# Moving an output projection's operand onto the finished scan's memory in a one-layer encoder trunk

## The chip, the cores and the metric

The kernel runs on one core of one Trainium2 chip. The metric is the device time of one execution in microseconds (us). The kernel before was timed three times: 1633.44, 1635.32 and 1642.16 us, a median of 1635.32 us. On this core TensorE (PE in the profile, with its weight loads as PEld) does the matrix products, VectorE (DVE), ScalarE (ACT) and GpSimd (POOL) do the elementwise work, and SyncE (SP) issues every DMA of this kernel from one queue. Each engine takes its instructions strictly in the order in which they were written into its stream, and waits at the first one whose inputs are not there.

## What is computed

One layer of a bidirectional encoder trunk on 1024 tokens of 1024 numbers, all in float32. Cut to what matters here:

```
h    = rms_norm(x) ; proj = h @ w_in
attn = window_attention(rope(q), rope(k), v)          # 512 of the mixer's 1024 columns
dn   = gated_deltanet(q, k, v, gate, decay, beta)     # the other 512, forward + backward scan
x    = x + rms_norm(concat(attn, dn) @ w_out)         # the output projection of the mixer
x    = x + rms_norm(cross_attention(rms_norm(x), mem) @ w_co)
gu   = rms_norm(x) @ w_gate_up
x    = x + rms_norm((silu(gate) * up) @ w_down)
```

Products are made to nearly float32 accuracy out of a fast matrix format: an operand is split into a rounded part `hi` and a remainder `lo`, and three products (hi·hi, hi·lo, lo·hi) are summed. The split is two instructions: a cast on ACT (`whi`, `b`, `s` ... at L102) and a subtraction on DVE or POOL (L103).

## The kernel before, in words

The program has three parts. The first makes all projections of the mixer and prepares the scans. The second (up to L934) runs the two delta-rule scans of 8 steps each, and around them, in an order written out by hand (`ORDER_3`), 16 windows of attention (8 blocks of 128 tokens for each of two groups of heads) and the keys and values of the memory tokens. Its last entries are windows and values: a window's scores (`psw`, L633) go through DVE (L635, maximum), ACT (L642, exponential; L650, scaling), a transposition on PE (`ptw`, L656), a split (`ph`, `pl`) and the product with the values (`pow`, L661), and its result `ao` is stored to the DRAM array `d_mix` (L666). The scans store their half of `d_mix` at L848. The values are products `pcv` (L907), copied out by ACT as `vv` (L911; that tile has one buffer) and stored to `d_mv` (L912).

The third part starts with the output projection of the mixer (`mid_gemm`, L994). It is done in two halves of 512 tokens (`hf` 0 and 1). Each half is 192 products of 512 columns in two chunks of columns; a chunk uses four blocks of `w_out`, 24 products each, and a block is loaded (`wraw`), cast (`whi`) and subtracted (`wlo`) in tiles that have two buffers each. The left operand of a half is `d_mix`, loaded in four blocks of 256 rows (`mraw`, L1033; block 0 and 1 are the two groups of the window attention, 2 and 3 the scans) and split into `b` tiles. Half 0 needs windows 0 to 3 of both groups, half 1 windows 4 to 7.

Where a tile lies decides when it can be written: a tile that is laid over another waits for the other's readers. The big operand tiles of part three (16 KB a partition each) lie in a pool `opB` (`b0`, `b1`, `b2`), in `opB3` (`b3`) on the left side of the memory, and in `opA` (`s00`, `s01`) on the right side, where the scans' tiles (pool `t3`) lay. In the kernel before, half 0 of the mixer's operand is `b1`, `b2`; its raw blocks 2 and 3 lie in `opA`, but raw blocks 0 and 1 lie in a separate pool `raw01` (L947) on the left, over memory that the windows use. Half 1 is `b0`, `b3`, its raw blocks in `opA`. The accumulators of the projection (`pg3`, four banks of PSUM) lie on the right side, where the windows' banks were, and two pools of two banks (`pn3`, `px3`) on the left, where the scans' and values' banks were.

A scheduler orders the instructions of each engine: it places them by its own estimate of when each could run, and weight loads are put ahead by `high_priority`. So moving a tile changes not only waits but the order in all five streams.

Behind the projection come the cross attention (`pcq`, `pcs`, `pco`), its output projection (the same `mid_gemm`), then the feed-forward part: 11 steps, each for two blocks of 128 gate columns and the same of up columns (index `i` 0 and 1), where products A, B, D, E of 12 matmuls each (L1165) are combined so that fewer products are needed. The last products of a step are the late ones, one each of A, D and E for both `i`; behind each of them `quarter` (L1235 to L1244) adds on DVE, takes the silu on ACT or multiplies by it on POOL. The down projection (`pd`) ends the kernel.

Of the kernel before, what the change touches and what calls it, by code (L numbers as in the profile page):

```python
# [10 lines left out]
F32 = mybir.dt.float32  # L11
F32R = mybir.dt.float32r
# [4 lines left out]
PSUM = bass.MemoryType.PSUM  # L17
DRAM = bass.MemoryType.DRAM

P = 128  # L20
S = 1024
D = 1024
KT = D // P
NT = S // P
HALF = 512
# [50 lines left out]
def tile_hybrid_block(  # L76
# [31 lines left out]
    def pool(name, bufs, **kw):  # L108
        return tc.tile_pool(name=name, bufs=bufs, reuse_waits="tile", **kw)
# [824 lines left out]


    p3 = ExitStack()
    pg = p3.enter_context(pool("pg3", 4, space=PSUM, side="right"))
    pn = p3.enter_context(pool("pn3", 2, space=PSUM))
    px = p3.enter_context(pool("px3", 2, space=PSUM))
    L0 = ExitStack()  # L940
    LX = ExitStack()
    opB = LX.enter_context(pool("opB", 1))
    b0, b1, b2 = (f"b{i}" for i in range(3))
    s2_first = [None] + [opB.tile([P, KT, HALF], F32R, tag=t, name=t) for t in (b0, b1, b2)]
    LR = ExitStack()
    raw01 = LR.enter_context(pool("raw01", 1)).tile([P, KT // 2, HALF], F32, name="mraw")
    LR.close()  # L947
    opB3 = LX.enter_context(pool("opB3", 1))
    opA = LX.enter_context(pool("opA", 1, side="right"))

# [72 lines left out]

    tz = L1.enter_context(pool("tz", 1))
    gp = gpost_tile(tz, g_mix_post)
    mxT = [s2_first[2:], [s2_first[1], opB3.tile([P, KT, HALF], F32R, tag="b3", name="b3")]]

    raws = [opA.tile([P, KT, HALF], F32, tag=f"s0{i}", name="mraw") for i in range(2)]
    for hf in range(2):
        for kp in range(4):  # L1030
            k2 = slice(2 * kp, 2 * kp + 2)
            raw = raw01 if hf == 0 and kp < 2 else raws[hf]
            nc.sync.dma_start(raw[:, k2, :], d_mix[kp * 256:(kp + 1) * 256, hf * HALF:(hf + 1) * HALF]  # L1033
                              .rearrange("(k p) t -> p k t", p=P))
            split(mxT[hf][0][:, k2, :], mxT[hf][1][:, k2, :], raw[:, k2, :])
    xn0 = mid_gemm(tz, mxT[0], w_out, gp, x, d_x1, 0)
    h2T = [operand(opA, "s0")]
    xn1 = mid_gemm(tz, mxT[1], w_out, gp, x, d_x1, 1, between=lambda: turn_norm(xn0, "cross", *h2T[0], pin=True))
    h2T.append(operand(opB, "s1"))
    turn_norm(xn1, "cross", *h2T[1])  # L1040

    mtp = L1.enter_context(pool("mtp", 1))
# [8 lines left out]
    tx = L2.enter_context(pool("tx", 2))  # L1051

    def cross_q(hf):
        q = operand(*((opB, "s2") if hf == 0 else (opA, "s0")))
        for ct in range(KT):
            whi, wlo = load_w(w_cq[:, ct * P:(ct + 1) * P], KT, P, nc.gpsimd)
            pp = [pg.tile([P, 512], F32, tag="pg", name="pcq")]
            gemm_b(whi, wlo, h2T[hf:hf + 1], pp)
            split(q[0][:, ct, :], q[1][:, ct, :], pp[0])
        return q  # L1060
# [60 lines left out]
    def blocks(t):  # L1121
        return t[:, 0:HK], t[:, HK:KT]

    xn = mid_gemm(tz, q0, w_co, gp, d_x1, d_x2, 0)
    x1h, x1l = operand(opB, "s1")
    X11, X21 = (x1h[:, 0:HK], x1l[:, 0:HK]), (x1h[:, HK:KT], x1l[:, HK:KT])

    def turned_k(xn, k):
# [7 lines left out]
        nc.scalar.activation(raw[:, k, :], pt, AF.Identity, scale=gain("ffn", k))  # L1136
        split(x1h[:, k, :], x1l[:, k, :], raw[:, k, :], eng=nc.gpsimd)
    xn = mid_gemm(tz, q1, w_co, gp, d_x1, d_x2, 1)
    T2, T4 = (blocks(t) for t in operand(opB, "s2"))
    T1, T3 = (blocks(t) for t in operand(opA, "s0"))  # L1140
    for k in range(HK):
        p0, p1 = turned_k(xn, k), turned_k(xn, k + HK)
        g0, g1 = gain("ffn", k), gain("ffn", k + HK)
# [28 lines left out]
    for e in range(EARLY):  # L1172
        f = 2 * e
# [74 lines left out]
    for f in range(0, NF, 2):  # L1248
        early = f // 2 < EARLY
        wts = [pair_weights(c0, early) for c0 in (f * P, FF + f * P)]  # L1250
        act = {(r, hf): tg.tile([P, HALF], F32, tag=f"act{r}{hf}", name=f"act{r}{hf}", bufs=1)
               for r in range(2) for hf in range(2) if not (early and r == hf == 0)}
        st = []
        for i, (W1, W22, (S1, S2, S3, S4)) in enumerate(wts):
            a1, v, u = (tg.tile([P, 512], F32, tag=n, name=n) for n in ("a1", "v", "u"))
            A = None
            if early:
                nc.sync.dma_start(a1, d_m1[f + i])
            else:
                A = bank("pA")  # L1260
                product(A, W1[0], X11)
                nc.scalar.copy(a1, A)
            B_, D_, E_ = (bank(n) for n in ("pB", "pD", "pE"))
            product(B_, S2, T2)
            nc.vector.tensor_tensor(v, a1, B_, ALU.add)
            product(D_, S1, T1)
            nc.vector.tensor_tensor(u, v, D_, ALU.add)
            product(E_, S3, T3)
            quarter(i, act, 1, 1, u, E_)
            st.append((A, D_, E_, v))  # L1270
        for i, (W1, W22, (S1, S2, S3, S4)) in enumerate(wts):
            A, D_, E_, v = st[i]
            if A is not None:
                product(A, W1[1], X21, start=False)
                quarter(i, act, 0, 0, None, A)
            product(D_, S4, X22, start=False)
            quarter(i, act, 0, 1, v, D_)
            product(E_, W22, T4, start=False)
            quarter(i, act, 1, 0, v, E_)
        for (r, hf), o_ in act.items():  # L1280
            nc.sync.dma_start(d_act[f + r][:, hf * HALF:(hf + 1) * HALF], o_)
# [99 lines left out]
```

## Time and profile before

The profiled execution took 1637.34 us on the device; its span, from the first instruction to the last, is 1635.6 us, so 1.7 us lie around it. It is 2.02 us above the median of the three timed runs.

| part of the span (us) | what runs | PE busy | granted clock |
|---|---|---|---|
| 400 to 560 | scans, windows, memory keys | 150.45 of 160.00 | 0.98 |
| 560 to 640 | last windows, memory values, start of the projection | 62.18 of 80.00 | 0.89 |
| 640 to 900 | projection, cross attention, second projection | nearly all | 0.94 to 1.00 |
| 1000 to 1100 | start of the feed-forward part | 97.42 of 100.00 | 1.00 |
| 1400 to 1636 | down projection | 227.40 of 236.00 | 0.99 |

In the lines of the profile each row of a timeline is a start, a duration, engine, line, operation, output and inputs, and in brackets the time for which the engine stood idle before it and what ended that. "Granted clock" is the share of full TensorE clock that the chip gave in a stretch; at 0.5 every product takes twice its time. The chain of waits is followed back from the last instruction, so whatever stands in it delayed the end.

### The profile page before, as it was taken

The numbers are of one execution on the slowest core, as the hardware profiler recorded it, in microseconds if no ns is written. First come the engines' busy times: TensorE is split into PE (matmuls) and PEld (weight loads), VectorE is DVE, ScalarE is ACT, GpSimd is POOL, SyncE is SP. The second block draws the span as 40 slices with busy tenths as digits, with TensorE's granted clock in tenths as the row PEclk, the third lists the DMA queues.
The fourth block names the chain that finished last, engine by engine and source line by source line (L and its number), as shares of the span: only waits on it lengthen the run. The fifth ranks groups of instructions, "written<-read, shape, count | busy, mean of one in ns | idle before, by whom it ended". The sixth has DMA issues, their size and how long they took to land.

```text
span 1635.6 us, 21442 instructions
## 1 busy us (share of the span) xinstructions
PE 1554.2 (95%) x7690; PEld 1301.3 (80%) x7690; DVE 942.7 (58%) x1431; ACT 750.8 (46%) x1518; POOL 548.9 (34%) x501
## 2 busy tenths in 40 slices
PE   6999889999899978999999999999999999999997
PEld 5878778777799857788888777888888888888886
DVE  6855986966668745443346458776555553334332
ACT  6556552237768764554336565233333232444211
POOL 2467553334337400253202221343333441321100
PEclk9999999898999998999999999999999999999999
DMA  6134257574999593454223164442223223565452
GB/s 201 41 116 130 64 166 208 140 181 133 320 320 289 149 293 112 151 184 146 74 65 116 52 213 151 126 135 77 78 90 96 79 84 114 202 214 183 140 175 73
DMA packets 267815, 240.47 MB, mean 147 GB/s; under 512 B 43176, under 2 KB 216637, under 8 KB 267709
## 3 DMA queue, kind: packets, MB, share of 16 engines
q1 hardware_dynamic: 267709, 239.11, 47.2%
q8 instruction: 60, 0.98, 0.3%
q14 instruction: 46, 0.38, 0.1%
HBM read 177.69 MB, written 58.75 MB: 145 GB/s over the span
## 4 chain that ended last, share of the span: by engine, by line
PE 67%; DVE 9%; DMA 6%; issue 3%; ACT 3%; POOL 2%; SPq 1%; POOLq 0%; ACTq 0%; DVEq 0%
PE pmg L994 10%; PE pd L1335 8%; PE pd L1311 7%; PE pE L1165 7%; PE pD L1165 7%; PE pA L1165 6%; PE pcq L260 5%; PE pB L1165 3%; PE psc L763 3%; PE pcs L1074 1%; PE pg L260 1%; DVE acc L285 1%; PE pco L1100 1%; PE pow L661 1%; DVE tmpb L510 1%
## 5 line engine op out<-in xcount | busy, mean ns | idle before, releaser
L102 ACT CAST whi<-wraw 128x1024 fp32r<-128x1024 f32 x108 | 113.4, 1050 | 167.3 <-issue 60.0
L103 POOL TENSOR_TENSOR wlo<-wraw,whi 128x1024 fp32r<-128x1024 f32 x48 | 118.3, 2464 | 174.4 <-ACT whi L102 156.1
L260 PE MATMUL pg<-hhi,whi 128*128 128x512 f32 x352 | 141.7, 404 | 0.2 <-ACT hhi L102 0.2
L260 PE MATMUL pg<-hlo,whi 128*128 128x512 f32 x352 | 141.5, 402 | 0.0
L260 PE MATMUL pg<-hhi,wlo 128*128 128x512 f32 x352 | 141.4, 402 | 0.0
L994 PE MATMUL pmg<-whi,b 128*128 128x512 f32 x384 | 119.8, 402 | 15.2 <-ACT b L102 12.6
L103 DVE TENSOR_TENSOR wlo<-wraw,whi 128x1024 fp32r<-128x1024 f32 x60 | 74.6, 1245 | 92.6 <-ACT whi L102 88.4
L1165 PE MATMUL pA<-b,whi 128*128 128x512 f32 x352 | 109.5, 392 | 1.4 <-ACT m L1182 1.4
L994 PEld LDWEIGHTS pmg<-whi,b 128*128 128x128 f32 x384 | 73.4, 193 | 32.1 <-ACT b L102 13.4
L285 DVE SCALAR_TENSOR_TENSOR acc<-cp,cols,acc 128x1024 f32<-128x1024 f32 x48 | 75.6, 1576 | 34.3 <-ACT acc L283 33.6
L1242 POOL TENSOR_TENSOR act<-act,up 128x512 f32<-128x512 f32 x33 | 48.4, 1468 | 106.6 <-issue 57.0
L260 PEld LDWEIGHTS pg<-hhi,wlo 128*128 128x128 f32 x352 | 68.0, 193 | 13.6
L260 PEld LDWEIGHTS pg<-hhi,whi 128*128 128x128 f32 x352 | 67.8, 193 | 13.5 <-ACT hhi L102 0.4
L260 PEld LDWEIGHTS pg<-hlo,whi 128*128 128x128 f32 x352 | 67.9, 193 | 13.3
L1165 PEld LDWEIGHTS pA<-b,whi 128*128 128x128 f32 x352 | 65.3, 188 | 15.1 <-ACT m L1182 2.0
L994 PE MATMUL pmg<-wlo,b 128*128 128x512 f32 x192 | 71.3, 392 | 0.0
L1165 PE MATMUL pA<-b,wlo 128*128 128x512 f32 x176 | 68.7, 391 | 1.1 <-DVE wlo L103 1.1
L1335 PE MATMUL pd<-wdh,ath 128*128 128x512 f32 x176 | 69.4, 395 | 0.0
L1335 PE MATMUL pd<-wdh,atl 128*128 128x512 f32 x176 | 69.4, 395 | 0.0
L1335 PE MATMUL pd<-wdl,ath 128*128 128x512 f32 x176 | 69.4, 395 | 0.0
L1311 PE MATMUL pd<-dl,whi 128*128 128x512 f32 x176 | 68.5, 389 | 0.0
L1311 PE MATMUL pd<-dh,wlo 128*128 128x512 f32 x176 | 68.3, 389 | 0.0
(392 smaller groups left out, 4145.0 us busy)
## 6 DMA issues: line engine op xcount, KB each, us to landing
wraw<-in_w_gate_up_dram SPq DMA_DIRECT2D x52, 512.0 KB, 3.9
kv<-d_kv SPq DMA_DIRECT2D x32, 512.0 KB, 7.1
wraw<-in_w_in_dram SPq DMA_DIRECT2D x22, 512.0 KB, 4.2
araw<-d_act SPq DMA_DIRECT2D x22, 512.0 KB, 3.4
draw<-in_w_down_dram SPq DMA_DIRECT2D x22, 512.0 KB, 4.3
atr<-d_act SPq DMA_DIRECT2D x16, 704.0 KB, 4.8
d_act<-act SPq DMA_DIRECT2D x40, 256.0 KB, 2.3
d_kv<-kv SPq DMA_DIRECT2D x8, 1024.0 KB, 6.4
```

The lines of the kernel that those rows point to most:

```text
L102: nc.scalar.copy(hi, src)
L103: (eng or nc.vector).tensor_tensor(lo, src, f32(hi), ALU.subtract)
L260: nc.tensor.matmul(p_, w[:, k, :], ah[a][:, k, :], start=(k == 0 and i == 0), stop=(k == nk - 1 and i == 2))
L285: nc.vector.scalar_tensor_tensor(acc, cp[:, t:t + S], taps[t], acc, ALU.mult, ALU.add)
L510: nc.vector.tensor_tensor(tv, A[:, j + 1:, j:j + 1].to_broadcast([P, n, j]), A[:, j:j + 1, 0:j].to_broadcast([P, n, j]), ALU.mult)
L661: nc.tensor.matmul(po.rearrange("p h t -> p (h t)"), vv[:, j].rearrange("p r e -> p (r e)"), pe_, start=(j == 0 and i == 0), stop=(j == nb ...
L763: nc.tensor.matmul(out[:, d, h, :], lt[:, d, h, :], rt[:, d, h, :], start=True, stop=True)
L994: nc.tensor.matmul(pp[t], act[a][:, k, tt], w_[:, kk, :], start=(k == 0 and i == 0), stop=(k == KT - 1 and i == 2))
L1165: nc.tensor.matmul(out_, w[a][:, k, :], xx[b_][:, k, :], start=(start and k == 0 and i == 0), stop=(k == HK - 1 and i == 2), skip_group_ch ...
L1242: nc.gpsimd.tensor_tensor(o_, o_, up, ALU.mult)
L1311: nc.tensor.matmul(pps[t], a[:, tt], b_, start=(f == 0 and i == 0), stop=(f == NF - 1 and i == 2))
L1335: nc.tensor.matmul(pp, a[:, f - f0], b_[:, f], start=(f == 0 and i == 0), stop=(f == NF - 1 and i == 2))
```

## The change

The first part of the diff changes places. Half 0 of the mixer's operand now lies in `opA`, over the scans' tiles, and its raw blocks all four in a pool `raw0` of its own on the right side, over the scans' tiles as well. Half 1's raw blocks lie in `b1`. The operands behind it move on in turn: the cross attention's inputs are `b1`, `b2` for half 0 and `opA` for half 1, its queries `s1` (`b0`, `b3`) and `s2` (`b1`, `b2`), and the feed-forward operands take `opA`, `s1`, `s2`. The accumulators' four banks go to the left side and the two small pools to the right.

The second part changes the order of the feed-forward part's late products: before, the late A, D and E of `i` = 0 and then those of `i` = 1; now both A, then both D, then both E.

```diff
-    pg = p3.enter_context(pool("pg3", 4, space=PSUM, side="right"))
-    pn = p3.enter_context(pool("pn3", 2, space=PSUM))
-    px = p3.enter_context(pool("px3", 2, space=PSUM))
+    pg = p3.enter_context(pool("pg3", 4, space=PSUM))
+    pn = p3.enter_context(pool("pn3", 2, space=PSUM, side="right"))
+    px = p3.enter_context(pool("px3", 2, space=PSUM, side="right"))
...
-    s2_first = [None] + [opB.tile([P, KT, HALF], F32R, tag=t, name=t) for t in (b0, b1, b2)]
-    LR = ExitStack()
-    raw01 = LR.enter_context(pool("raw01", 1)).tile([P, KT // 2, HALF], F32, name="mraw")
-    LR.close()
+    opB_first = [opB.tile([P, KT, HALF], t, tag=n, name=n) for n, t in ((b0, F32R), (b1, F32), (b2, F32R))]
...
-    mxT = [s2_first[2:], [s2_first[1], opB3.tile([P, KT, HALF], F32R, tag="b3", name="b3")]]
-
-    raws = [opA.tile([P, KT, HALF], F32, tag=f"s0{i}", name="mraw") for i in range(2)]
+    mxT = [operand(opA, "s0"), [opB_first[0], opB3.tile([P, KT, HALF], F32R, tag="b3", name="b3")]]
+    LR = ExitStack()
+    raws = [LR.enter_context(pool("raw0", 1, side="right")).tile([P, KT, HALF], F32, name="mraw"), opB_first[1]]
     for hf in range(2):
         for kp in range(4):
             k2 = slice(2 * kp, 2 * kp + 2)
-            raw = raw01 if hf == 0 and kp < 2 else raws[hf]
+            raw = raws[hf]
             nc.sync.dma_start(raw[:, k2, :], d_mix[kp * 256:(kp + 1) * 256, hf * HALF:(hf + 1) * HALF]
                               .rearrange("(k p) t -> p k t", p=P))
             split(mxT[hf][0][:, k2, :], mxT[hf][1][:, k2, :], raw[:, k2, :])
+    LR.close()
     xn0 = mid_gemm(tz, mxT[0], w_out, gp, x, d_x1, 0)
-    h2T = [operand(opA, "s0")]
+    h2T = [[opB.tile([P, KT, HALF], F32R, tag=b1, name=b1), opB_first[2]]]
...
-    h2T.append(operand(opB, "s1"))
+    h2T.append(operand(opA, "s0"))
...
-        q = operand(*((opB, "s2") if hf == 0 else (opA, "s0")))
+        q = operand(opB, ("s1", "s2")[hf])
...
-    x1h, x1l = operand(opB, "s1")
+    x1h, x1l = operand(opA, "s0")
...
-    T2, T4 = (blocks(t) for t in operand(opB, "s2"))
-    T1, T3 = (blocks(t) for t in operand(opA, "s0"))
+    T2, T4 = (blocks(t) for t in operand(opB, "s1"))
+    T1, T3 = (blocks(t) for t in operand(opB, "s2"))
...
-        for i, (W1, W22, (S1, S2, S3, S4)) in enumerate(wts):
-            A, D_, E_, v = st[i]
+        for i, (A, D_, E_, v) in enumerate(st):
             if A is not None:
-                product(A, W1[1], X21, start=False)
+                product(A, wts[i][0][1], X21, start=False)
                 quarter(i, act, 0, 0, None, A)
-            product(D_, S4, X22, start=False)
+        for i, (A, D_, E_, v) in enumerate(st):
+            product(D_, wts[i][2][3], X22, start=False)
             quarter(i, act, 0, 1, v, D_)
-            product(E_, W22, T4, start=False)
+        for i, (A, D_, E_, v) in enumerate(st):
+            product(E_, wts[i][1], T4, start=False)
             quarter(i, act, 1, 0, v, E_)
```

In the five streams of the built programs this stands as follows. On SP, all four raw blocks of half 0 are now issued before the last three windows (before: two of them, and three of half 1), and the four of half 1 behind the last window's store; the load of the memory keys for the cross attention (`mkr`, 1 MB) goes behind one more block of value weights, and the load of the memory values (`mvr`, 1 MB) ahead of half 1's blocks. On ACT and DVE, the four casts and four subtractions of half 0 stand among the last three windows (before: behind them). The third weight block's cast stands behind the cast of the memory keys, the fourth's behind the cast of the memory values and the first cast of half 1. On PE, the first product of the projection follows the last window's products but for two that are mixed in a little later, and the last value products stand ahead of the last two windows' value products. The numbers of matmuls, casts, subtractions and DMAs are the same.

## The prediction

> **What bounds the kernel now.** I read the page first, its busy times and its chain of waits.
>
> ```profile
> PE 1554.2 (95%) x7690; PEld 1301.3 (80%) x7690; DVE 942.7 (58%) x1431; ACT 750.8 (46%) x1518; POOL 548.9 (34%) x501
> ...
> PE 67%; DVE 9%; DMA 6%; issue 3%; ACT 3%; POOL 2%; SPq 1%; POOLq 0%; ACTq 0%; DVEq 0%
> ```
>
> TensorE is busy for 95% and is two thirds of the chain, so time can come only from where it stands still or runs slowly. The view of waits, for PE from 600 to 700 us, and the busy times by stretch show the one large place.
>
> ```profile
> PE pmg L994 <- ACT b L102: 12.4, 1, 12.4
> ...
> 592.00:596.00 4.00, 4.00 (x16) 3.27 (x15) 1.75 (x2) 2.14 (x6) 0.00 (x0) 0.57 1.07 366
> 596.00:609.00 13.00, 9.74 (x46) 7.70 (x44) 6.20 (x6) 7.54 (x12) 0.00 (x0) 1.00 0.63 191
> 609.00:618.00 9.00, 0.00 (x0) 0.00 (x0) 3.25 (x3) 8.04 (x8) 0.00 (x0) 0.51 0.93 286
> 618.00:623.00 5.00, 4.49 (x10) 3.11 (x11) 4.91 (x5) 2.98 (x4) 0.00 (x0) 0.52 0.50 202
> 623.00:640.00 17.00, 17.00 (x77) 14.03 (x76) 9.18 (x7) 4.80 (x6) 0.00 (x0) 1.00 0.20 64
> ```
>
> The columns are busy time of PE, PEld, DVE, ACT, POOL, then granted clock, DMA share, GB/s. From 609 to 618 PE does nothing; from 618 to 623 it works at half the clock (10 products in 4.49 us, where 77 take 17.00 afterwards). PE's timeline gives the exact ends, and the chain says why:
>
> ```profile
> 605.35 0.39 PE L661 MATMUL pow<-ph,vlo 128*128 128x512 f32 x1
> 618.10 2.08 PE L994 MATMUL pmg<-whi,b 128*128 128x512 f32 x4 [12.36 <-ACT b L102]
> ...
> 622.87 0.39 PE L994 MATMUL pmg<-whi,b 128*128 128x512 f32 x1
> ```
> ```profile
> 605.54 4.35 DMA d_mv<-vv
> ...
> 609.97 0.59 ACT vv L911
> ...
> 611.44 6.86 DMA mraw<-d_mix
> ...
> 619.32 1.23 DVE b L103
> ...
> 620.59 43.75 PE pmg L994 x187
> ...
> 1376.80 2.72 PE pA L1165 x12
> ```
>
> The projection's first half waits for the last two of its raw blocks, issued only after the windows and behind a store of values, then for their split. After that PE is full: the first half's products run through, and so does the feed-forward part, at 2.72 / 12 = 0.227 us a matmul.
>
> **The change part by part.** *Removed: the wait.* From 605.35 to 622.87 are 17.52 us, in which 11 matmuls start (the last of the windows and the 10 of the row from 618 to 623). At 0.227 us they need 2.5 us. So 15.0 us can go: 12.4 of standing still, the rest half clock and a last wait for DVE. With half 0 loaded and split before the last window ends, nothing of it remains.
>
> *Moved ahead: loads, casts and subtractions among the last three windows.* The durations, and the time that ACT has there:
>
> ```profile
> L102 ACT CAST b<-mraw x8: 1043/1045/1047, 610.4 to 619.7; 128x1024 fp32r<-128x1024 f32 x8
> L103 DVE TENSOR_TENSOR b<-mraw,b x8: 1218/1219/1226, 611.6 to 625.2; 128x1024 fp32r<-128x1024 f32 x8
> ...
> DMA to landing us min/median/max: 6.8/8.2/9.6
> ```
> ```profile
> 585.98 0.41 ACT L621 CAST vhi<-vr 128x256 fp32r<-128x256 f32 x1 [2.31 <-PE pow L661]
> ...
> 595.73 1.05 ACT L102 CAST whi<-wraw 128x1024 fp32r<-128x1024 f32 x1 [1.86 <-DMA wraw<-in_w_ckv_dram]
> ...
> 610.45 4.83 ACT L102 CAST b<-mraw 128x1024 fp32r<-128x1024 f32 x5
> 618.32 1.05 ACT L102 CAST b<-mraw 128x1024 fp32r<-128x1024 f32 x1 [0.27 <-DMA mraw<-d_mix]
> 619.66 1.04 ACT L102 CAST b<-mraw 128x1024 fp32r<-128x1024 f32 x1 [0.30 <-DMA mraw<-d_mix]
> ...
> 622.16 1.91 ACT L102 CAST vr<-mvr 128x2048 fp32r<-128x2048 f32 x1 [1.45 <-DMA mvr<-d_mv]
> ```
>
> Back to back five casts take 4.83 us, so four take 3.9 us. Each waits for its load with ACT's queue behind it: the windows' casts `ph` and exponentials, for which PE waits. The subtractions, 4 × 1.22 = 4.9 us, stand in DVE's queue ahead of the windows' maxima and `pl`. Upper bound: all 3.9 us on the windows' path (DVE's overlap ACT's by one step). Lower bound: below nothing, because SP's queue gets shorter there. One 512 KB load less and the 1 MB key load stand ahead of the value weights; loads in a row land 619.66 − 618.32 = 1.34 us apart, so these weights land some 4 us earlier, and the 1.86 us for which ACT stood idle for them can go: −1.9. I take 2.5 us, nearer to the upper end: the windows are a chain through three engines, and idle time of ACT in it (2.31 us at 585.98) is mostly time in which the chain is elsewhere, so an inserted cast delays it as often as not. The stores and loads moved past on SP cost issue time alone, while the queue has other loads to move. The key load now also waits for the fourth subtraction (it lies over half 0's raw tile); behind it on SP stand the last value weight and the stores, but that weight waits for a buffer until then anyway. POOL's queue does not change in this stretch.
>
> *Made late in turn: the projection's third and fourth weight blocks.* A block is 24 matmuls, 5.44 us. ACT casts the fourth one behind the memory values (1.91 us) and half 1's first cast (0.97), and the memory values are loaded only when the last `vv` has been stored. Upper bound: the load lands as before, 622.16 − 605.35 = 16.8 us after the last window product; then 1.91 + 0.97 + 0.97 + 1.23 (subtraction) = 21.9 us, against a need 3 × 5.44 = 16.3 us after the start: 5.6 us of standing still. Lower bound nothing: the load stood behind three others of 1.34 us (now they stand behind it), which is 4.0 us less, and in the new order ten matmuls of the windows stand behind the last value product (before: two), which with their waits is about the 1.6 us that then lack. I take 1.0 us, near the lower end, because both reasons are in the order of the built program.
>
> *Moved behind: half 1's four loads, casts and subtractions.* They have the 43.75 us of half 0's products as cover and cost nothing; without it, four loads 1.34 us apart after 8.2 us, a cast and a subtraction would be some 14.5 us.
>
> *The other operands and the banks* cost nothing: each new place was last read by work that stands well ahead on PE's queue (the queries' place by the projection's second half, written after it), and the first accumulators wait for copies of banks that ACT does ahead of the last `ph` on which PE waits anyway.
>
> *The late gate products.*
>
> ```profile
> 1100.00:1200.00 100.00, 100.00 (x443) 82.81 (x442) 58.59 (x71) 32.00 (x50) 43.52 (x27) 1.00 0.26 81
> 1200.00:1400.00 200.00, 200.00 (x885) 165.58 (x884) 95.98 (x122) 59.75 (x91) 67.09 (x44) 1.00 0.30 97
> ```
> ```profile
> L1237 ACT ACTIVATE act<-act x24: 629/633/637, 1101.0 to 1377.6; 128x512 f32<-128x512 f32 x24
> L1242 POOL TENSOR_TENSOR act<-act,up x24: 1281/1295/1750, 1113.7 to 1385.9; 128x512 f32<-128x512 f32 x24
> L1235 DVE TENSOR_TENSOR act<-u,pE x8: 678/680/689, 1100.3 to 1357.8; 128x512 f32<-128x512 f32 x8
> ```
>
> PE is full, and the same matmuls in another order fill it as well. The gate's add and silu (0.68 + 0.63 us) now have one product, 2.72 us, before the multiply needs them, which still covers them; the multiply, 1.30 us, has no product behind it in its step. If the cover failed at each of 11 steps, 11 × 1.3 = 14 us; but a step's four early products of each index stand between, so I take 0. The first steps, where PE is busy for 97.42 of 100 us, have DVE as their limit, which does the same work.
>
> *The sum.* 15.0 − 2.5 − 1.0 = 11.5 us off. Behind 640 us the rest moves up as it is. The profiled execution took 1637.34 us, so 1625.8 by it; it lay 2.02 us above the median of the three runs, so 1623.8 us against the median of 1635.32.
>
> [...] PE's clock halved from 592 to 596 (0.57), after a gap that one row shows:
>
> ```profile
> 590.42 0.49 PE L661 MATMUL pow<-ph,vhi 128*128 128x512 f32 x1 [2.33 <-ACT ph L102]
> ```
>
> [...] By the row such a spell comes again, as before, and the sum stays; I go by the row.
>
> **The rivals.** *Half of it given back* (0.13): the windows' path takes the full 3.9 us and the fourth weight block the full 5.6: 15.0 − 9.5 = 5.5 off, 1629.8. For it speaks that a load takes up to 9.6 us where the queue is full; against it that both are upper bounds from a fuller queue.
>
> *Nothing happens* (0.07): the first product starts early but PE waits as long for its weights or banks, so that the stretch to the fourth block has its old length: 1635.3. For it: weights were on the chain ahead of the gap too (the 1.86 us above). Against it: two blocks were cast before the gap in the kernel before, and their places do not change.
>
> *Slower* (0.06): ACT's queue starves the windows so that PE falls to half clock for the whole last stretch. Its place is 582 to 609; the price is the 9.5 us above and the work at half clock: PE's 9.74 us from 596 to 609, and the like before 592,
>
> ```profile
> 582.00:592.00 10.00, 7.09 (x38) 5.51 (x37) 4.55 (x15) 7.11 (x20) 0.93 (x2) 1.00 1.05 391
> ```
>
> 7.09 us, once more: 16.8. Together 26.3 against 15.0: 11.3 us slower, 1646.6. It decides from 15.0 us of such delay on. For it: the row at 592 shows how little idle time halves the clock. Against it: ACT is busy for only 7.11 of 10 us there, so 3.9 us more do not starve it.
>
> **How the numbers follow.** The forecast has the rest, 0.74. Its own range is the bounds: 15.0 + 1.9 = 16.9 off, 1618.4, up to 0.5% off, 1627.1 (about what a measurement of this kernel tells from no change: the three runs shown lie 0.5% apart). The range of 1618 to 1631 takes in the first rival and leaves out the other two, 0.13. Faster by over 0.5%: the forecast, 0.74; within: the first two rivals, 0.20; slower: 0.06.
>
> **What would show it.** Right: PE's wait for `b` at the first projection product falls from 12.4 us to under 1; that product starts at 606 to 610 us, at granted clock near 1; the stretch behind ends some 11 us earlier, all of it moved alike. The windows' end moves from 605.35 to about 608 (step two); PE waits for the fourth block's `whi` by about 1 us (step three). Late gates: PE still full from 1100 to 1400. Wrong: a gap of PE before 606, or at the third or fourth block, of over 5 us, a half clock from 582 on, or PE idle between the feed-forward steps.

## The result, and the profile after

The changed kernel took 1627.88 us (median of 20 runs, 1622.88 to 1633.36) where the kernel before took 1636.8 beside it: a ratio of 0.9948, 95% interval 0.9937 to 0.9959. A second series on another occasion gave 1625.81 us and 0.9938 (0.9919 to 0.9956). It is faster by half a per cent: 8.9 and 11.6 us, where 11.5 was forecast. The profiled execution took 1627.8 us, its span is 1626.1.

The busy times by stretch of the changed kernel, the same five stretches as in the prediction (columns PE, PEld, DVE, ACT, POOL, granted clock, DMA share, GB/s):

```profile
592.00:596.00 4.00, 3.73 (x19) 3.19 (x20) 2.25 (x7) 2.40 (x6) 0.90 (x2) 1.00 0.97 334
596.00:609.00 13.00, 11.17 (x56) 8.38 (x54) 6.98 (x10) 11.10 (x26) 0.00 (x0) 1.00 0.66 200
609.00:618.00 9.00, 9.00 (x40) 7.45 (x41) 4.59 (x4) 4.96 (x6) 0.00 (x0) 1.00 0.84 264
618.00:623.00 5.00, 5.00 (x24) 4.14 (x23) 3.88 (x4) 3.49 (x4) 0.00 (x0) 1.00 0.89 298
623.00:640.00 17.00, 16.66 (x74) 13.46 (x73) 9.02 (x10) 6.84 (x13) 0.00 (x0) 1.00 0.46 156
```

From 609 to 618 PE is busy for all 9.00 us at full clock, where it did nothing before. The view of waits for PE, 600 to 700 us, and the rows of PE's timeline at the start of the projection and at the end of its first chunk:

```profile
PE pmg L991 <- ACT whi L102: 2.2, 1, 2.2
PE pow L661 <- ACT ph L102: 1.1, 1, 1.1
PE pow L661 <- ACT ao L665: 0.4, 1, 0.4
PE pmg L991 <- DVE z L995: 0.3, 1, 0.3
```
```profile
608.98 0.50 PE L661 MATMUL pow<-ph,vhi 128*128 128x512 f32 x1 [1.14 <-ACT ph L102]
609.31 0.63 PE L991 MATMUL pmg<-whi,s 128*128 128x512 f32 x2
...
631.33 0.39 PE L991 MATMUL pmg<-wlo,s 128*128 128x512 f32 x1
632.06 0.73 PE L991 MATMUL pmg<-whi,s 128*128 128x512 f32 x2 [0.34 <-DVE z L995]
```

The wait of 12.4 us for `b` is gone. What is left are a wait of 2.2 us for `whi` (664 us; it was there before, at 675; from one product's start to the next it is 2.62 us, below called the gap at 664), a new one of 0.3 us for `z`, and one of 1.1 us for the last window's `ph`. ACT's rows show what `ph` stood behind:

```profile
607.27 1.05 ACT L102 CAST whi<-wraw 128x1024 fp32r<-128x1024 f32 x1 [0.45 <-DMA wraw<-in_w_out_dram]
608.34 0.58 ACT L102 CAST ph<-ptw 128x512 fp32r<-128x512 f32 x1
```

It is the cast of a projection weight block, which had waited 0.45 us for its load, while the input of `ph` was done at 606.48 us. The four casts of half 0's operand were over by 589.3 us.

Times since the start of the span mislead here: one row of SP's timeline from each kernel shows why (the load of the gains, the last point up to which both programs issue the same).

```profile
570.82 0.42 SPq L971 DMA_DIRECT2D gpost<-in_g_mix_post_dram  x1
```
```profile
573.39 0.42 SPq L968 DMA_DIRECT2D gpost<-in_g_mix_post_dram  x1
```

The changed kernel's profiled execution was 2.57 us late before anything had changed. So the table below compares stretches: from that load to the first projection product (`pmg`), from there to the first query product (`pcq`), and from the first B product of the feed-forward part to the first `pd`. Each is a difference of two starts in one trace (before: 618.10 − 570.82 = 47.28). The ratios are to runs of the kernel before on the same chip; its median there lay between 1635.67 and 1637.45 us. The stretch between, from `pcq` to the first A product, is 239.15 to 239.18 us in every trace but one; from the first A to the first B product it is 50.75 to 52.60; the down projection is 250.74 to 250.85.

| kernel | median us | ratio to before (95%) | load to `pmg` | `pmg` to `pcq` | B to `pd` |
|---|---|---|---|---|---|
| before | 1636.8 | | 47.28 | 97.39 | 378.56 |
| changed | 1627.88 | 0.9948 (0.9937 to 0.9959) | 35.92 | 94.33 | 381.07 |
| changed, again | 1625.81 | 0.9938 (0.9919 to 0.9956) | 36.73 | 97.04 | 381.35 |
| late products by index | 1621.93 | 0.9906 (0.9889 to 0.9922) | 35.41 | 97.31 | 379.19 |
| the same, again | 1622.9 | 0.9910 (0.9886 to 0.9934) | 35.75 | 96.42 | 379.57 |
| by kind in the later steps only | 1623.32 | 0.9913 (0.9896 to 0.9930) | 35.73 | 95.67 | 378.97 |
| before, late products by kind | 1640.14 | 1.0021 (1.0006 to 1.0035) | 47.09 | 96.99 | 383.42 |
| changed, banks as before | 1630.71 | 0.9956 (0.9940 to 0.9973) | 38.53 | 97.09 | 382.94 |
| before, banks turned | 1636.58 | 1.0005 (0.9985 to 1.0025) | 47.41 | 97.55 | 378.49 |
| by index, half 0's casts doubled | 1621.85 | 0.9914 (0.9893 to 0.9934) | 37.38 | 96.08 | 379.22 |
| by index, scaling on DVE | 1620.05 | 0.9906 (0.9885 to 0.9927) | 36.02 | 92.68 | 379.41 |
| by index, half 0's scaling on DVE | 1620.84 | 0.9898 (0.9873 to 0.9923) | 37.40 | 92.41 | 378.75 |
| that, half 1's subtractions on POOL | 1622.04 | 0.9909 (0.9894 to 0.9924) | 36.05 | 92.78 | 378.71 |

Between the two profiled executions the load-to-`pmg` stretch gives 11.36 us, the next 3.06, and the feed-forward part takes 2.51 back; with 0.18 us from the others that is 12.1 us, and 2.57 of late start leave the 9.5 us by which the spans differ. The second execution of the changed kernel gives 8.3 us in place of the 12.1. The loss in the feed-forward part is one gap. PE's and DVE's rows there, in the changed kernel:

```profile
1040.82 0.62 PE L1163 MATMUL pD<-x,s3h 128*128 128x512 f32 x2
...
1043.31 0.39 PE L1163 MATMUL pD<-x,s3l 128*128 128x512 f32 x1
...
1045.28 0.68 DVE L1265 TENSOR_TENSOR u<-v,pD 128x512 f32<-128x512 f32 x1
...
1046.10 0.70 PE L1163 MATMUL pD<-x,s3h 128*128 128x512 f32 x2 [2.40 <-DVE u L1265]
```

and in the kernel before, at the same step:

```profile
1052.93 0.62 PE L1165 MATMUL pD<-x,s3h 128*128 128x512 f32 x2
...
1056.92 0.68 DVE L1267 TENSOR_TENSOR u<-v,pD 128x512 f32<-128x512 f32 x1
...
1058.37 0.62 PE L1165 MATMUL pD<-x,s3h 128*128 128x512 f32 x2
```

The late D of index 1 adds to the bank from which `u` of index 1 is read, so it waits for `u`. Before, `u` was done 4.67 us after the late D of index 0 had begun (1056.92 + 0.68 − 1052.93), and two products, 5.44 us (1058.37 − 1052.93), stood ahead of the late D of index 1. With the products by kind only one stands there, 2.72 us.

### The profile page after: what moved, and what is told of

It is laid out like the page before. It is cut to its first block, busy times and chain, and to the rows that moved or that the text cites. A ratio compares the mean times of both kernels' runs of the same rounds, so it can differ in the third digit from the quotient of the medians.

```text
span 1626.1 us, 21448 instructions
## 1 busy us (share of the span) xinstructions
PE 1554.1 (96%) x7690; PEld 1298.7 (80%) x7690; DVE 940.8 (58%) x1431; ACT 747.7 (46%) x1518; POOL 543.8 (33%) x501
## 4 chain that ended last, share of the span: by engine, by line
PE 67%; DVE 10%; DMA 6%; issue 3%; ACT 3%; POOL 1%; SPq 1%; POOLq 0%; ACTq 0%; DVEq 0%
PE pmg L991 10%; PE pd L1334 8%; PE pd L1310 7%; PE pE L1163 6%; PE pD L1163 6%; PE pA L1163 6%; PE pcq L260 5%; PE pB L1163 3%; PE psc L763 3%; PE pg L260 3%; DVE acc L285 1%; DVE A L512 1%; PE pcs L1072 1%; DVE tmpb L510 1%; PE pco L1098 1%
## 5 line engine op out<-in xcount | busy, mean ns | idle before, releaser
L1163 PE MATMUL pA<-s,whi 128*128 128x512 f32 x352 | 109.5, 392 | 1.4 <-ACT m L1180 1.4
L1240 POOL TENSOR_TENSOR act<-act,up 128x512 f32<-128x512 f32 x33 | 44.3, 1345 | 112.3 <-issue 59.0
L1163 PEld LDWEIGHTS pA<-s,whi 128*128 128x128 f32 x352 | 65.3, 188 | 15.1 <-ACT m L1180 2.0
L1212 POOL TENSOR_TENSOR sr<-wraw 128x512 f32<-128x512 f32 x22 | 28.4, 1291 | 124.8 <-DMA wraw<-in_w_gate_up_dram 118.1
L1163 PE MATMUL pA<-s,wlo 128*128 128x512 f32 x176 | 68.8, 392 | 1.1 <-DVE wlo L103 1.1
```

The lines of the kernel that those rows point to most:

```text
L1163: nc.tensor.matmul(out_, w[a][:, k, :], xx[b_][:, k, :], start=(start and k == 0 and i == 0), stop=(k == HK - 1 and i == 2), skip_group_ch ...
L1212: nc.gpsimd.tensor_tensor(s[0], b_[:, 0:HK], b_[:, HK:], ALU.add)
L1240: nc.gpsimd.tensor_tensor(o_, o_, up, ALU.mult)
```

## The experiments

**The second part undone, and done alone.** First the change with the late products by index again (the loop of the kernel before, in the changed kernel):

```diff
-        for i, (A, D_, E_, v) in enumerate(st):
-            if A is not None:
+        for i, (W1, W22, (S1, S2, S3, S4)) in enumerate(wts):
+            A, D_, E_, v = st[i]
+            if A is not None:
...
-        for i, (A, D_, E_, v) in enumerate(st):
-            product(D_, wts[i][2][3], X22, start=False)
+            product(D_, S4, X22, start=False)
...
-        for i, (A, D_, E_, v) in enumerate(st):
-            product(E_, wts[i][1], T4, start=False)
+            product(E_, W22, T4, start=False)
```

> The change without its second part: places and banks as changed, the late products by index again, as before. Theory (the order of the late products costs 2.6 us: the late D of index 1 comes one product earlier and waits 2.4 us for u in one early step): the gap of 2.79 us at the fourth early step is gone, 2.6 us under the changed kernel, about 1625.3 us and a ratio to the kernel before of 0.993. Rival (the early steps are short of weights and the gap only shows where they run out): a gap of 2 to 3 us stands at another product between 1030 and 1060 us, the time is that of the changed kernel, 1627.9 us, ratio 0.9948.

> The kernel before with the second part alone (late products by kind). Theory: a gap of PE ahead of the late D of index 1 in the early steps; in the kernel before u of index 1 is done 4.67 us after the late D of index 0 starts, and one product takes 2.72, so 2.0 to 2.4 us slower than before, ratio 1.0013. Rival (weights): no difference from before, ratio 1.000, PE without a gap of over 1.5 us from 1030 to 1070 us. The forecast (0 for this part) stands with the rival.

The second kernel is the one before with the changed loop alone. PE's busy time from 1030 to 1060 us with late products by index, and then PE's waits from 1030 to 1070 in the kernel before with products by kind:

```profile
1030.00:1060.00 30.00, 29.79 (x131) 24.10 (x130) 21.23 (x27) 7.71 (x13) 11.85 (x9) 1.00 0.48 151
```
```profile
PE pD L1165 <- DVE u L1267: 3.0, 1, 3.0
PE pB L1165 <- ACT s1h L102: 0.2, 1, 0.2
```

By index the gap is gone and none takes its place; by kind alone brings it to the kernel before (3.0 us of waiting, the feed-forward stretch 378.56 to 383.42, the time 2.7 us up, interval 1.0 to 5.7). The rival, weights that run short whatever the order, falls. The stretch from the first A to the first B product differs between traces too; from the first A product to the first `pd`, the four traces with products by kind in the early steps take 432.55 to 435.66 us and the nine others 430.15 to 431.91. The median by index is 6 us under the changed kernel, more than the expected 2.6, so it was run again:

> Late products by index with the rest of the change, once more, beside the others on one chip. Theory: 1622 us, ratio 0.9906; 35.4 to 36.7 us from the issue of the gain load to the first projection product; feed-forward stretch 379 us; the gap of 2.62 us comes again, and a spell of half clock behind it if one span of the grid holds so much of it that PE is busy in it for under 0.55, so that the projection stretch is 95.7 to 97.3 us, and 94.3 if the gap is shared by two spans. Rival (the 6 us under the changed kernel were the chip's or the hour's): 1625 us, ratio 0.993.

1622.9 us: the intervals of both series lie below that of the changed kernel's first series (they overlap with its second, and the last still takes in the rival's 0.993). So the gain came again, but the medians leave its size at 3 to 6 us. From the first A product to the first `pd`, the changed kernel's two traces are 0.6 to 1.3 us longer than these two. Half clock behind the gap can make it dearer (below), but neither trace of the changed kernel has it there; what exceeds the gap stays open.

**Where by kind costs.** In the changed kernel, by index in the four early steps (they have no late A products), by kind in the others:

```diff
-        for i, (A, D_, E_, v) in enumerate(st):
+        kinds = [(i, c) for i in range(2) for c in "ADE"] if early else [(i, c) for c in "ADE" for i in range(2)]
+        for i, c in kinds:
+            A, D_, E_, v = st[i]
...
```

> The change with the late products by index in the four early steps and by kind in the other seven. Theory (by kind costs where the late product comes too early after u, which is in an early step, and nothing where PE is full): as the changed kernel with all late products by index, 1625.3 us, ratio 0.993, no gap at 1040 and PE full from 1100 to 1400 us. Rival one (by kind also costs in the later steps): between that and the changed kernel, with gaps there. Rival two (by kind gains something in the later steps that the gap hid): over 1 us under the other one.

1623.32 us and 378.97 us for the feed-forward stretch, as with all of it by index (379.19, 379.57), and PE full in the rest of it:

```profile
1060.00:1400.00 340.00, 340.00 (x1502) 281.53 (x1501) 176.58 (x221) 104.68 (x164) 123.67 (x81) 1.00 0.31 99
```

So the order matters in the early steps alone; in the later ones by kind neither costs nor gains.

**The banks.** The changed kernel with the banks as before, and the kernel before with the banks turned:

```diff
-    pg = p3.enter_context(pool("pg3", 4, space=PSUM))
-    pn = p3.enter_context(pool("pn3", 2, space=PSUM, side="right"))
-    px = p3.enter_context(pool("px3", 2, space=PSUM, side="right"))
+    pg = p3.enter_context(pool("pg3", 4, space=PSUM, side="right"))
+    pn = p3.enter_context(pool("pn3", 2, space=PSUM))
+    px = p3.enter_context(pool("px3", 2, space=PSUM))
```

> The change with the PSUM banks of the projections as before (four accumulators on the right, where the windows' banks were, the two pairs on the left). Forecast's view: the banks cost and bring nothing, 1627.9 us, ratio 0.9948, PE goes from the windows to the projection without a gap of over 1 us. Rival (the places alone would not remove the wait, since the accumulators then wait for the copies out of the windows' last banks): a gap of 2 to 4 us ahead of the first projection product, perhaps a half clock behind it, 1630 to 1632 us, ratio 0.996 to 0.997.

> The kernel before with the PSUM banks turned alone; all five instruction streams keep their order. Theory (the place of the raw blocks sets the wait): first projection product 12.4 to 12.8 us behind the last window product as before, 1637 us, ratio 1.000. Rival (the banks are worth 2.6 us by themselves, as the changed kernel with the old banks suggests: 38.53 us from the issue of the gain load to the first projection product, against 35.92): 44.7 us instead of 47.3 for that stretch, ratio 0.998.

PE's timeline around the first projection product, with the banks back:

```profile
607.72 0.50 PE L661 MATMUL pow<-ph,vhi 128*128 128x512 f32 x1 [0.91 <-ACT ph L102]
608.97 0.50 PE L661 MATMUL pow<-pl,vhi 128*128 128x512 f32 x1 [0.75 <-DVE pl L103]
609.31 0.40 PE L661 MATMUL pow<-ph,vlo 128*128 128x512 f32 x1
609.55 0.63 PE L991 MATMUL pmg<-whi,s 128*128 128x512 f32 x2
```

and in the kernel before with the banks turned:

```profile
604.14 0.39 PE L661 MATMUL pow<-ph,vlo 128*128 128x512 f32 x1
616.43 0.79 PE L994 MATMUL pmg<-whi,b 128*128 128x512 f32 x1 [11.91 <-ACT b L102]
```

Turned alone, the banks do nothing: the operand sets the wait. With the operand in its new place they are worth something. With the banks back the scheduler puts the first projection product behind all three products of the last window, so PE waits for `pl` with nothing to do; with them turned it stands behind the first of the three (608.98 and 609.31 in the changed kernel), and two of the window's products, 0.46 us, come later. The stretch is 38.53 us against 35.92 and 36.73: 2.2 and 1.3 us net of these 0.46. The trace with the banks back has one spell of half clock in this stretch, as has the one of 36.73, and the one of 35.92 has none; so like for like it is 1.3 us, from one trace each. By the median it is 2.8 us, with intervals that overlap. The gap of 2 to 4 us that the rival expected ahead of the first projection product did not come: two waits of 0.9 and 0.8 us stand there. Behind it PE waits once more in this version, at its third weight block, whose cast stands behind that of the memory values:

```profile
PE pmg L991 <- ACT whi L102: 0.9, 1, 0.9
...
PE pmg L991 <- DVE wlo L103: 0.4, 1, 0.4
```

**What a cast among the windows costs.** Late products by index, and each block of half 0 cast once more, into the tile that the subtraction overwrites:

```diff
             raw = raws[hf]
...
+            if hf == 0:
+                nc.scalar.copy(mxT[0][1][:, k2, :], raw[:, k2, :])
             split(mxT[hf][0][:, k2, :], mxT[hf][1][:, k2, :], raw[:, k2, :])
```

> The change with late products by index, and half 0's four casts doubled (each block is cast into the remainder's tile first, where the subtraction overwrites it): 3.9 us more of ACT among the last windows. It tells what such a cast costs the windows' path. By the forecast's price (2.5 of 3.9 us): the stretch from the issue of the gain load to the first projection product takes 38 us instead of 35.4, 2.5 us slower than with late products by index alone. If the price is what the changed kernel showed (0.7 to 1.2 of 3.9 us): 36.1 to 36.7, about 1 us slower. By the upper bound: 39.3, 3.9 us slower.

The stretch to `pmg` took 37.38 us, between the 38 of the forecast's price and the 36.1 to 36.7 of the changed kernel's, so it doesn't decide between them. Half clock moves this stretch as well. In the eight traces with the new places and banks and no extra casts, it is 35.41 to 36.05 us in the six without half clock in it, 36.73 in the one with one span of 3.41 us, and 37.40 in the one with two. The version with the extra casts has one: against 36.73 the casts cost 0.65 us, from one trace each, and against the six 1.33 to 1.97. In either case it is less than the forecast's 2.5 and far from 3.9; whether the casts also brought the spell is open. The time, 1621.85 us, shows no difference; one us is less than its interval tells.

**The changed kernel again, for its clock.**

> The changed kernel once more, beside the others on one chip. In five of the six traces so far the gap of 2.62 us in the projection's second half (664 us in the changed kernel) was followed by 3.4 us at half clock; in the changed kernel's it was not. Theory (the missing spell was chance, by the phase of that execution): here it comes, the stretch from the first projection product to the first query product takes 96 to 97.3 us instead of 94.33; and a spell behind the gap at the fourth feed-forward step is as likely, so that the late order costs 2.1 us without it and 4.4 with it. Rival (the changed kernel's clock is steadier by itself): 94.3 us again and no spell behind either gap. Time 1626 to 1630 us, ratio 0.995, in both.

Busy times in stretches of 3.41 us, the changed kernel's first execution (first two rows around the gap at 664, the third over the gap at 1043):

```profile
662.47:665.89 3.42, 2.54 (x12) 1.77 (x10) 0.00 (x0) 3.42 (x6) 1.48 (x4) 1.00 0.14 55
665.89:669.30 3.41, 2.06 (x9) 1.71 (x10) 2.08 (x2) 2.25 (x3) 0.00 (x0) 1.00 0.00 0
...
1041.36:1044.78 3.42, 2.34 (x11) 1.61 (x9) 3.39 (x6) 2.02 (x4) 0.32 (x1) 1.00 0.01 3
```

and its second:

```profile
659.47:662.89 3.42, 1.18 (x6) 0.86 (x5) 1.07 (x1) 3.26 (x4) 0.20 (x1) 1.00 0.00 0
662.89:666.30 3.41, 3.41 (x10) 2.64 (x9) 1.29 (x2) 0.00 (x0) 0.00 (x0) 0.50 0.55 163
...
1038.42:1041.83 3.41, 1.65 (x8) 1.03 (x6) 3.38 (x6) 1.76 (x3) 0.00 (x0) 1.00 0.13 37
1041.83:1045.24 3.41, 2.54 (x11) 2.15 (x12) 3.31 (x5) 0.63 (x1) 1.29 (x1) 1.00 0.61 194
```

The same gap of 2.6 us is followed by 3.41 us at half clock in the second execution and by none in the first. In the second it lies in one span of that length (PE busy for 1.18 of 3.42 us); in the first it is shared by two (2.54 and 2.06). The last section has the shares. So the missing spell was chance, as expected, and the `pmg`-to-`pcq` stretch is 97.04 us with it. Behind the gap at the fourth feed-forward step, where a spell was expected to be as likely, none came in either execution. The last two rows show it for the second (they lie 0.07 us behind the spans by which half clock came in this execution): PE is busy for 1.65 us in one and 2.54 in the other.

**The gap at 664, closed.** The projection's second half waits for `whi`. ACT's row says what it does at that time, in the changed kernel:

```profile
664.07 2.19 ACT L1011 ACTIVATE xr<-z,pr 128x1024 f32<-128x1024 f32 x2
666.16 1.98 ACT L102 CAST whi<-wraw 128x1024 fp32r<-128x1024 f32 x2
```

The cast stands behind the scaling of half 0's normed rows. First the scaling of both halves on DVE, then that of half 0 alone (with `if hf == 0`):

```diff
-            nc.scalar.activation(xr, z, AF.Identity, scale=r2)
+            nc.vector.tensor_scalar(xr, z, r2, None, ALU.mult)
```

> The change with late products by index, and the scaling of the normed rows (L1011) on DVE instead of ACT, where the casts of the projection's weight blocks stand behind it. Theory: the gap of 2.62 us in the projection's second half falls under 1 us and the half clock behind it goes too, so the stretch from the first projection product to the first query product is about 93.3 us instead of 95.7 to 97.3, 4 us under late products by index. [...] Rival two (DVE, now with the scaling ahead of the weight subtractions, is late instead): a gap at another block, no gain.

> As the last one (scaling of the normed rows on DVE), but for the first half of each projection alone; the second half's stays on ACT, because the two gaps of 1.3 us that the last kernel had at 707 and 710 us stand behind the second half's. Theory: the projection stretch stays at 92.7 us, the one behind it falls from 241.49 to 239.17 us, 1617.8 us, 2.3 under the last one. Rival (the scheduler moves more than this, or the second half's rows on ACT bring a gap back): 1620 us. Half clock, by what the ten traces show (it comes in spans of 3.41 us that lie on one grid in each execution, and follows a span of that grid in which PE is busy for under about 0.55): no spell between 600 and 1600 us, unless a gap leaves such a span.

PE's busy time with both on DVE, first over the place of the gap and then behind the projection:

```profile
650.00:670.00 20.00, 20.00 (x89) 16.33 (x88) 12.62 (x15) 9.36 (x17) 8.16 (x11) 1.00 0.58 195
...
697.00:730.00 33.00, 31.13 (x153) 25.59 (x153) 19.54 (x18) 15.53 (x26) 18.65 (x16) 1.00 0.51 168
```

and with half 0's alone:

```profile
650.00:670.00 20.00, 20.00 (x89) 16.28 (x88) 13.01 (x15) 9.98 (x18) 9.47 (x11) 1.00 0.53 187
...
697.00:730.00 33.00, 33.00 (x164) 27.69 (x163) 13.64 (x16) 20.96 (x31) 20.28 (x18) 1.00 0.56 184
```

Gap and half clock are gone in both, as the theory had it (PE busy for 20.00 of 20.00 us at clock 1.00). The first gives 2.3 us back at 707 and 710 us, where transpositions wait for `xr` from DVE (the stretch behind takes 241.49 us instead of 239.17): rival two holds for that part. In the second's trace nothing is given back. The medians are 1620.05 and 1620.84 us, 1 to 3 us under late products by index where 2.4 to 4 were expected, and 5 to 8 under the changed kernel. Against late products by index the intervals of the ratios overlap, so this gain is shown by the traces, not by the times. That the second beats the first, as its trace has it, doesn't show in the medians: it was expected at 1617.8 us and came out at its rival's 1620. These two have the lowest medians of all that were run.

**The new wait for `z`.** DVE's queue at the end of half 0's first chunk, in the changed kernel:

```profile
629.05 1.22 DVE L103 TENSOR_TENSOR wlo<-wraw,whi 128x1024 fp32r<-128x1024 f32 x1
630.18 1.22 DVE L103 TENSOR_TENSOR b<-b,b 128x1024 fp32r<-128x1024 f32 x1
631.32 1.88 DVE L995 TENSOR_TENSOR z<-pmg,gpost 128x512 f32<-128x512 f32 x3
```

The second chunk's products need the banks that `z` reads, and half 1's last subtraction stands ahead of that. To take it away, half 1's subtractions went to POOL (on top of half 0's scaling on DVE):

```diff
-            split(mxT[hf][0][:, k2, :], mxT[hf][1][:, k2, :], raw[:, k2, :])
+            split(mxT[hf][0][:, k2, :], mxT[hf][1][:, k2, :], raw[:, k2, :], eng=nc.gpsimd if hf else None)
```

> As the last but one (scaling of half 0's normed rows on DVE), and half 1's four subtractions on POOL, which is idle from 600 to 650 us, instead of DVE. It tells what PE waits for behind half 0's first chunk of columns (0.3 us in the changed kernel, 0.2 to 1.8 us in the others, for DVE's reading of the accumulators, z). Theory (DVE reads the accumulators late because half 1's last subtraction stands ahead of that on its queue): the wait is under 0.2 us, the stretch from the first projection product to the first query product 0.7 us under the 92.41 of the last but one, about 91.7. Rival one (it is ACT, which squares the accumulators behind half 1's last cast): the wait stays at 0.5 to 1 us. Rival two (POOL's subtractions are twice as long, so half 1's operand is late): a wait of PE for b at the second half's first product.

```profile
627.46 5.74 POOL L103 TENSOR_TENSOR b<-b,b 128x1024 fp32r<-128x1024 f32 x2 [1.64 <-ACT b L102]
...
628.37 2.57 DVE L103 TENSOR_TENSOR wlo<-wraw,whi 128x1024 fp32r<-128x1024 f32 x1 [4.80 <-ACT whi L102]
...
629.31 0.60 ACT L994 ACTIVATE z<-pmg 128x512 f32<-128x512 f32 x1
...
630.87 1.87 DVE L995 TENSOR_TENSOR z<-pmg,gpost 128x512 f32<-128x512 f32 x3
```

These are rows of that kernel's timeline, POOL, DVE and ACT. The wait is 1.2 us where under 0.2 was expected (0.7 without this edit), and nothing was gained: DVE's own subtraction took 2.57 us instead of 1.22 while POOL's ran. It is still DVE's queue that is late, not ACT, whose pass over the first bank began at 629.31 and took 0.60: rival one falls. Rival two falls too: POOL took 2.87 us for each subtraction, but PE didn't wait for `b` at the second half's first product. That half 1's subtraction causes the wait is read from the order of DVE's queue; this run doesn't show it, and how much it costs stays open.

## Why the prediction was right, and where not

*The number.* The medians are 8.9 and 11.6 us under the kernel before, and the traces 12.1 and 8.3 from the load of the gains on, where 11.5 was forecast. The forecast's direction and its main mechanism, the wait for half 0's operand, were right. That the sum came out as near as it did is partly luck: a loss that it had put at nothing stands against a gain that it had put at nothing, and half clock behind a gap came in one execution and not in the other. The first series, 1627.88 us, lies just above the forecast's own bound of 1627.1, between its 1623.8 and the first rival's 1629.8; but the 5.6 us of waiting for the fourth weight block that this rival needs are in no trace.

*What is removed* was right in place and size. From 609 to 623 PE is now full at clock 1.00, and the start of the projection moved by 11.36 and 10.55 us where the forecast's numbers (12.5 of waiting less 2.5) give 10.0; 0.46 us of window products come later.

*Loads and casts among the last windows*, forecast at 2.5 us: the sum came out near it, if like is compared with like. In the three traces with the old places, each with one span of half clock in the windows, the windows are through 34.76, 34.89 and 35.34 us after the load of the gains (for the first: 47.28 less the 12.75 from the start of the last window product to the first of the projection, plus that product's 0.23). In the changed kernel's second execution, with one such span, it is 36.73 and 0.46 us of window products: 1.9 to 2.4 us more. In its first, without half clock there, it is 35.92 and 0.46, 1.0 to 1.6 more; the forecast had expected a spell. With the banks as before and one span it is 38.52, 3.2 to 3.8 us more. So the size holds with the banks' gain in it, and would have been too small without. Its working missed something, though. The forecast put half 0's four casts, 3.9 us, on the windows' path. From the load of the gains to the last `ph`, ACT in fact had 6.1 us more to do than before (27.5 instead of 21.4): two casts of weight blocks and one copy of values had moved ahead of it as well, and the last window waits behind one of these casts. The doubled casts cost less than the forecast's price, 0.65 us like for like. So the nearness is in part luck, and how the sum divides among these instructions isn't shown.

*The fourth weight block*: forecast 1.0 us of waiting for its `whi`. With the banks turned no trace has that wait; with the banks as before there are 0.9 us for `whi` and 0.4 for `wlo`, at the third block. Instead PE waits 0.2 to 1.8 us for `z` at the start of the second chunk. That this is about the forecast's size is luck, as the wait is another. Half 1's loads, casts and subtractions, which the forecast called free, are a likely cause, since a subtraction stands ahead of the accumulators' reading in DVE's queue; that isn't shown. The cover of 43.75 us was there for half 1's operand, but says nothing of what is queued behind it.

*The banks* at nothing: wrong by about 1.3 us to the good, like for like. "The first accumulators wait for copies of banks that ACT does ahead of the last `ph`" missed that the scheduler also orders PE by these banks.

*The late products* at nothing: this term failed. The forecast asked whether the gate's add, silu and multiply are covered, looked for the answer from 1100 on, and found it rightly for the later steps (PE full from 1060 to 1400). For the early steps it said that DVE "does the same work". It didn't look at how close DVE's `u` comes ahead of the late D: 5.44 − 4.67 = 0.77 us of slack, which one product of 2.72 us overdraws by 1.95 (in the changed kernel's trace the wait was 2.40). PE idle between the feed-forward steps was one of the forecast's own signs of being wrong, and it came. The four traces with products by kind in the early steps show a gap of 2.8 to 3.4 us there, two of them with half clock behind it. Their stretch is 2.5 to 4.9 us longer than in the kernel before; of that 0.2 to 1.0 stand in the versions of the change by index too. By index the medians are 14.4 and 15.5 us under the kernel before, more than forecast; the two traces, 10.6 and 10.7 us from the load of the gains on, show less. So that the late products cost time is shown, and where; how much of the medians' difference is theirs is not.

*The clock.* The forecast went by one row (half clock from 592 us behind a gap of 2.33 us) and expected a spell among the windows again. In the changed kernel's two executions there was none and one. By the traces the length of a gap alone doesn't settle it: PE was busy for 1.45 us of the 3.41 us ahead of that spell in the kernel before, and none of the changed kernel's spans of that length on its own grid, from 560 to 1600 us in the first execution, has less than 1.60 (the last section has the shares).

## What to carry to other kernels

Where a write waits for a read of the same bank, take the slack from the profile before (when is the reader done, how many products stand between) for the stage in which supply is tightest, not for the one in which the engine is full. A transfer or split that is hidden for its own reader still stands in a queue: look at what is behind it there. And compare two profiled executions by stretches between the same instructions, since their starts can differ (here by up to 7.2 us in five executions, where the change was worth 8.9 and 11.6).

## What the hardware showed that was not expected

*Half clock comes on a grid.* In the traces of the kernel before and of the changed kernel's first execution the spells of half clock begin at whole multiples of 3.413 us from each other (within 0.003 us in a trace, by the starts of the granted clock's records) and last one to four such spans, but for the last, behind the end of the products (7.89 and 6.45 us). Cut on that grid, from 560 to 1600 us, every span of these two in which PE was busy for a share of up to 0.43 was followed by half clock, and none from 0.47 up. In four other traces, spans with 0.12, 0.33, 0.35 and 0.53 were followed by one at clock 0.50, and one with 0.48 was not. (From 300 to 420 us, among other products, even a span in which PE counts as busy throughout was followed by half clock, 386.04 to 389.45 us in the changed kernel; why is open.) Behind the projection's gap of 2.6 us half clock came in nine of the ten traces that have it (`pmg` to `pcq` 95.67 to 97.55 us in these) and not in the tenth (94.33), where two spans share the gap. The price of a spell of 3.41 us where PE is full is an estimated 1.7 us (half of 3.41). So removing this gap was worth, by that estimate, up to 1.7 us more than its length.

*One program, other starts.* The changed kernel and the versions with another late order issue the same instructions up to the fourth early step, yet the gain load went out between 566.22 and 573.39 us in five executions. What makes it is open. The half clock ahead of that point adds up to 41.0 to 54.6 us in these five, and the two latest have the most (47.8 and 54.6), so it may be a part of it.

*A subtraction on DVE took longer beside one on POOL.* One of 128x1024 took 2.57 and 2.59 us on DVE while one of the same size ran on POOL, against 1.22 us in the changed kernel, where POOL ran none there.
